# First stage with silu of c on one row and plain column sums; feed-forward and delta net tiles moved to the address of hh modulo 1024

## The chip, the cores and the metric

One core of one Trainium2 chip runs the whole program in one launch. The metric is device time in microseconds (us), the median of the runs of one kernel. Engines are named as the profile names them: PE is TensorE (PEld its weight loads), DVE is VectorE, ACT is ScalarE, POOL is GpSimd, SP is SyncE, whose queue issues nearly all DMAs.

## The reference, cut to what matters

```python
def rms_norm(x, g):
    y = x * lax.rsqrt(jnp.mean(x * x, axis=-1, keepdims=True) + EPS)
    return y * g

def swiglu_ffn(h, w_in, w_out):
    gate, up = jnp.split(h @ w_in, 2, axis=-1)
    return (jax.nn.silu(gate) * up) @ w_out

def reference(x, c, ...):              # x (1, 512, 1024), c (1, 1024), d_ff 2816
    cs = jax.nn.silu(c)
    for i in range(2):
        mod = (cs @ w_ada[i] + b_ada[i]).reshape(B, 3, 3, D)   # shift, scale, gate of three sub-layers
        h = rms_norm(x, norm_g[i, 0]) * (1 + mod[:, 0, 1]) + mod[:, 0, 0]
        x = x + 0.5 * (1 + mod[:, 0, 2]) * swiglu_ffn(h, w_ffn_in[i, 0], w_ffn_out[i, 0])
        h = rms_norm(x, norm_g[i, 1]) * (1 + mod[:, 1, 1]) + mod[:, 1, 0]
        x = x + (1 + mod[:, 1, 2]) * (conv_module(h, ...) if i == 0 else gated_deltanet(h, ...))
        h = rms_norm(x, norm_g[i, 2]) * (1 + mod[:, 2, 1]) + mod[:, 2, 0]
        x = x + 0.5 * (1 + mod[:, 2, 2]) * swiglu_ffn(h, w_ffn_in[i, 1], w_ffn_out[i, 1])
    return rms_norm(x, final_g)
```

## The kernel before, in words

Activations stand transposed: 128 partitions are features, the free axis is the 512 tokens, and the 1024 features are 8 slices `k`. Every product of a large weight is made of three matmuls in fp32r (`mm3`): weight and activation are each split into a high part (`whi`, `hh`) and a remainder (`wlo`, `hl`), and PE adds `whi*hh`, `whi*hl` and `wlo*hh` (lines 172 to 174). Each weight block of 128 columns is loaded by SP into `raw`, cast by ACT into `whi` (line 163), and DVE subtracts to get `wlo` (line 164).

The program has six stages one after the other: feed-forward, convolution module, feed-forward, feed-forward, delta net, feed-forward. In a feed-forward, the pairs of blocks of `w_fi` multiply `hh`, `hl`; their products, split into `ahi` and `alo`, are multiplied by `w_fo` in three groups of 7, 7 and 8 slices (`GROUPS`). The last two of the eight output blocks of the third group, and the head of the next stage, are done in two halves of 256 tokens (`tail`), so that matmuls are 512 or 256 columns wide. The delta net's output product does the same with its tile `ohl`. Inside these stages the order on each engine is the order in which the code is written (`manual_schedule`).

The first stage is written apart (`begin`, and the lines above it). SP loads `c`, `x` in four pieces of two slices, constants, and then for each `k` the rows of the adaLN weights for scale and shift (`load_ada`, two transfers of 512 KB into four places of `stage`) and the first seven weight blocks of slice `k` (`load_st`, 448 KB, two places). The row `c` is multiplied by a column of ones on PE, which lays it on all 128 partitions; ACT takes silu of it into `cs` (128 x 1024). ACT squares the slices of `x`, DVE adds the first six, and PE multiplies the sum and the last two squares by a 128 x 128 matrix of 1/1024 (`mean`), so that each partition has the mean square of each token. ACT takes the square root and DVE the reciprocal of all 128 x 512 elements (`rstd`). For each slice `k` DVE multiplies a row of the adaLN weights by `cs` and sums (`shape`, one call for scale and one for shift), scales `x` (`unit`) and makes the remainders (`low`, `lower`); ACT makes `hh` and its fp32 twin (`high`); and PE runs 21 matmuls into seven accumulators:

```python
        for k in range(KT):
            high(k); cast(k + 1); shape(1, k + 1); low(k); shape(0, k + 1)
            unit(k + 1); lower(k + 1); load(k + 2)
            # 14 matmuls whi, wlo with hh[k], then 7 whi with hl[k]
```

A place in `stage` is loaded anew only when DVE and ACT have read it, and SP takes its DMAs in order. The addresses of tiles are given out by pools in the order in which tiles are asked for. `hh`, `hl` and all slots of `whi` and `wlo` lie at byte 832 modulo 1024 in each partition (a slice of a weight block is 512 bytes, so its slices lie at 832 and 320).

Of the kernel before, what the change touches and what calls it, by code (L numbers as in the profile page):

```python
# [7 lines left out]
F32 = mybir.dt.float32  # L8
F32R = mybir.dt.float32r
BF16 = mybir.dt.bfloat16  # L10
AF = mybir.ActivationFunctionType
ALU = mybir.AluOpType
# [3 lines left out]
P = 128  # L16
T = 512
H2 = T // 2
D = 1024
# [27 lines left out]
NMC = 4  # L47
CT = [3,5]
ARB = 3
SCK = [0,2]  # L50
SNW = 7
NSD = 6
NSH = 3
UMB = 3
HALO=8
# [51 lines left out]
def trunk_kernel(ctx: ExitStack, tc: tile.TileContext, x_in, c_in, vecs, consts, w_ada, w_st,  # L107
# [11 lines left out]
    def nm(s):  # L119
        n_name[0] += 1  # L120
        return f"{s}_{n_name[0]}"
# [4 lines left out]
    def aux_tile():  # L126
        return psum.tile([P, T], F32, tag="ps", name=nm("aux"))

    def scratch(tag, shape=(P, T), dt=F32, bufs=1):
        return sc.tile(list(shape), dt, tag=tag, name=nm(tag), bufs=bufs)  # L130
# [231 lines left out]
            evac(ps, m, full)  # L362

    def preload(func, dep):
        act.activation(scratch("dum", (P, 1)), dep, func, bias=eps, scale=0.0)

    def tok_rstd(pt, n, scale, tag):
        st = scratch(tag, (P, n), bufs=2)
# [10 lines left out]
    def col_sum(pt, src, col0, step=1):  # L379
        for g in range(src.shape[1] // P):  # L380
            pe.matmul(pt[:, col0 + g * step:col0 + g * step + 1], src[:, g * P:(g + 1) * P], ones, start=True, stop=True)
# [109 lines left out]
    def ffn(layer, which, nxt, first=None):  # L491
        sub = 2 * which
        f = layer * 2 + which
        norm = Norm()
        ng = len(GROUPS)
        with tc.tile_pool(name=nm("ffn"), bufs=1) as ap, ExitStack() as ax:
            pump = bool(ada["plan"])
            rate = APACE[which]
            if pump:
                ada["raw"] = ax.enter_context(tc.tile_pool(name=nm("adar"), bufs=2))  # L500
            done = SNW if first else len(edge["w"])
            srcs, starts = [], []
            j0 = 0
            for n in GROUPS:
                starts.append(j0)
                srcs += [(w_fi[f, i], KT) for i in range(max(2 * j0, done), 2 * (j0 + n))]
                srcs += [(w_fo[f, m, :, j0:j0 + n, :], n) for m in range(KT)]
                j0 += n
            srcs += [(s, KT) for s in (nxt[2][:2] if nxt else [])]
            feed = Feed(srcs, [] if first else edge["w"][len(edge["ps"]):], not first)  # L510
            begun = first(f, ap, feed) if first else edge["ps"]
            region = ax.enter_context(ExitStack())
            region.enter_context(tc.manual_schedule(engines=ENG))
            box = {}
            for _ in range(2):
                feed.prep()

            def step(n):
                if pump:
                    ada_step(n)  # L520

            def block(nk, mhi, mlo):
                feed.prep()
                w = feed.take()
                ps = mm_tile()
                for k in range(nk):
                    mm3(ps, w, k, mhi[:, k, :], mlo[:, k, :], k == 0, k == nk - 1)
                return ps

            def glu_a(g):  # L530
                box["s"] = s = scratch("sil", bufs=2)
                act.activation(s, g, AF.Silu)  # L532

            def glu_b(u):
                box["pr"] = pr = scratch("t", bufs=2)
                dve.tensor_tensor(pr, box["s"], u, ALU.mult)  # L536

            def glu_c(jj):
                pr = box["pr"]
                act.copy(ahi[:, jj, :], pr)  # L540
                dve.tensor_tensor(alo[:, jj, :], pr, ahi[:, jj, :].bitcast(F32), ALU.subtract)  # L541

            for gi, n in enumerate(GROUPS):
                ahi = ap.tile([P, n, T], F32R, tag="ahi", name=nm("ahi"))
                alo = ap.tile([P, n, T], F32R, tag="alo", name=nm("alo"))
                for jj in range(n):
                    if len(begun) > 1:
                        g, u = begun.pop(0), begun.pop(0)
                        glu_a(g)
                    else:  # L550
                        g = begun.pop(0) if begun else block(KT, hh, hl)
                        step(rate[0])
                        glu_a(g)
                        u = block(KT, hh, hl)
                        step(rate[1])
                    glu_b(u)
                    glu_c(jj)

                if gi == ng - 1:
                    ev = resid(norm, layer, sub)  # L560
                    for m in range(KT - 2):
                        ps = block(n, ahi, alo)
                        step(rate[2])
                        ev(ps, m, full)
                    if pump:
                        ada_drain(which == 1)
                    tail(None, n, ahi, alo, layer, sub, norm, nxt, feed)
                else:
                    ev = plain_resid(layer, sub)
                    for m in range(KT):  # L570
                        ps = block(n, ahi, alo)
                        step(rate[2])
                        ev(ps, m, full)
# [361 lines left out]
    def deltanet(layer, nxt):  # L935
        NU = HEADS * NG
        norm = Norm()
        with tc.tile_pool(name=nm("dn"), bufs=1) as dp, \
                tc.tile_pool(name=nm("spill"), bufs=1, space=bass.MemoryType.DRAM) as dd:
            kq = dp.tile([P, HEADS, NG, 4, CH], F32, tag="b1", name="kq")  # L940
            kt = dp.tile([P, NG, HEADS, P], F32, tag="b2", name="kt")
            da = dp.tile([P, HEADS, NG, CH], F32, tag="s1", name="da")
            dt = dp.tile([P, HEADS, NG, CH], F32, tag="s2", name="dt")
            am = dp.tile([P, NU, CH], F32, tag="s3", name="am")
            tok = dp.tile([P, NG, 16], F32, name="tok")
            gc = dp.tile([P, HEADS, NG], F32, name="gc")
            egl = dp.tile([P, HEADS, NCH], F32, name="egl")
            kds = dp.tile([P, HEADS, NG], F32, name="kds")
            nbe = dp.tile([P, HEADS, NG], F32, name="nbe")
            beta = dp.tile([P, HEADS, NG], F32, name="beta")  # L950
            ssk = dp.tile([P, HEADS, NG], F32, name="ssk")
# [456 lines left out]
            so = dp.tile([P, 2, HEADS, P], F32, tag="s2", name="so")  # L1408
            S, o0 = so[:, 0], so[:, 1]
            pool.memset(o0[:CH], 0.0)  # L1410
            rms = dp.tile([P, 5, HEADS], F32, name="rms")
            lo_r, hi_r = slice(0, CH), slice(CH, P)

            def oslot(s):
# [132 lines left out]
    orow = ada["pool"].tile([1, P], F32, name="orow", bufs=1)  # L1547
    dve.memset(orow, 1.0)
    nc.sync.dma_start(crow, c_in)
    for k in range(0, KT, 2):  # L1550
        nc.sync.dma_start(x[:, k:k + 2, :], x_in[:, k:k + 2, :])
    nc.sync.dma_start(ident, consts[:, :P])
    nc.sync.dma_start(vec[:, :V1], vecs[:, :V1])
    preload(AF.Silu, eps)
    pcs = [aux_tile() for _ in range(2)]
    for j in range(2):
        pe.matmul(pcs[j], orow, crow[:, j * T:(j + 1) * T], start=True, stop=True)
    mean = ada["pool"].tile([P, P], F32, name="mean", bufs=1)
    dve.memset(mean, 1.0 / D)
    rstd0 = ada["pool"].tile([P, T], F32, name="rstd0", bufs=1)  # L1560
    pt0 = aux_tile()
    sums = scratch("ssum", bufs=1)
    for k in range(KT):
        if k == 0:
            act.activation(sums, x[:, k, :], AF.Square)
        else:
            sq = scratch("sq", bufs=2)
            act.activation(sq, x[:, k, :], AF.Square)
            if k < NSD:
                dve.tensor_tensor(sums, sums, sq, ALU.add)  # L1570
            if k == NSD - 1:
                pe.matmul(pt0, mean, sums, start=True, stop=False)
            if k >= NSD:
                pe.matmul(pt0, mean, sq, start=False, stop=k == KT - 1)
        if k in SCK:
            j = SCK.index(k)
            act.activation(cs[:, j * T:(j + 1) * T], pcs[j], AF.Silu)
            if j:
                preload(AF.Sqrt, cs[:, D - 1:])

    def begin(f, ap, feed):
        stage = ap.tile([P, 4 * D + 2 * SNW * P], F32, tag="ahi", name="stage")
# [31 lines left out]
        def shape(kind, k):  # L1614
            if k < KT:
                c = kind * KT + k
                m = mod[:, 0, c:c + 1]
                junk = ada["raw"].tile([P, D], BF16, tag="ajunk", name=nm("ajunk"), bufs=1)
                dve.tensor_tensor_reduce(junk, adas[kind, k], cs, 1.0, 0.0, ALU.mult, ALU.add, accum_out=m)
                act.activation(m, m, AF.Identity, bias=V("b_ada", c))  # L1620
                if kind:
                    act.activation(gain[:, k:k + 1], m, AF.Identity, scale=V("norm_g", k), bias=V("norm_g", k))

        def unit(k):
            if k < KT:
                xn[k] = scratch("t", bufs=2)
                dve.tensor_tensor(xn[k], x[:, k, :], rstd0, ALU.mult)

        def high(k):
            g, b = gain[:, k:k + 1], mod[:, 0, k:k + 1]  # L1630
# [6 lines left out]

        load(0)
        load(1)
        act.activation(rstd0, pt0, AF.Sqrt, bias=eps)  # L1640
        cast(0)
        dve.reciprocal(rstd0, rstd0)
        unit(0)
        shape(1, 0)
        shape(0, 0)
        ps = [mm_tile() for _ in range(SNW)]
        lower(0)
        for k in range(KT):
# [132 lines left out]
```

## Time and profile before

| | |
|---|---|
| median of 3 runs (lowest, highest) | 2063.96 us (2063.76, 2065.14) |
| the profiled execution's own time | 2064.65 us |
| its span, first to last instruction | 2062.8 us |
| PE busy | 1997.0 us, 97% of the span |
| DVE, ACT, POOL busy | 57%, 38%, 10% |
| first matmul of the first feed-forward | 25.55 us after the span's start |

The profiled execution is one run, 0.69 us above the median. Busy shares are averages over stages; a matmul's listed duration contains its way through the pipeline, so the rate of PE is read from the distance between the starts of matmuls, not from that duration. Of matmuls a few records can be missing.

### The profile page before, as it was taken

Reading aid. Unit: us, or ns where it says so; the run is one execution under the profiler, and the core shown is the slowest. Engines: PE = TensorE matmul, PEld = TensorE weight load, DVE = VectorE, ACT = ScalarE, POOL = GpSimd, SP = SyncE. Lnnn points to the kernel's source line nnn. Section 1 sums busy time; section 2 is a strip of 40 time slices with the busy share of each in tenths; the row PEclk is TensorE's granted clock in tenths of the full one; section 3 lists DMA queues with packets and bytes.
Section 4 is the critical chain, followed back from the end, with each engine's and each line's share of the span. In section 5 each row is a group of like instructions: output and inputs, shape, how many; then the busy total and the mean of one; then the engine's idle time right before and its main releaser. Section 6 shows DMA issues by size and latency. Waiting matters only on the chain.

```text
span 2062.8 us, 26172 instructions
## 1 busy us (share of the span) xinstructions
PE 1997.0 (97%) x10330; PEld 1669.5 (81%) x10330; DVE 1174.2 (57%) x1815; ACT 789.1 (38%) x1357; POOL 198.2 (10%) x139
## 2 busy tenths in 40 slices
PE   6999999998899999999999999999799999999998
PEld 4888888887898888888888888887677798888887
DVE  6766667799865656536333333576745664333334
ACT  5422222475542222224322222377556643222222
POOL 0000000299200000000000000024210100000000
PEclk9999999999899999999999999999999999999999
DMA  7767676322136656532333323322221133333331
GB/s 263 242 219 241 225 237 227 117 82 92 52 112 204 214 182 211 169 99 68 113 99 92 103 93 102 113 72 72 62 63 35 49 113 99 99 98 93 102 93 62
DMA packets 78333, 262.06 MB, mean 127 GB/s; under 512 B 8321, under 2 KB 14081, under 8 KB 78082
## 3 DMA queue, kind: packets, MB, share of 16 engines
q1 hardware_dynamic: 77666, 259.87, 39.6%
q8 instruction: 81, 1.33, 0.3%
q10 hardware_dynamic: 544, 0.52, 0.1%
q14 instruction: 42, 0.34, 0.1%
HBM read 254.59 MB, written 5.77 MB: 126 GB/s over the span
## 4 chain that ended last, share of the span: by engine, by line
PE 87%; DVE 5%; POOL 3%; ACT 3%; issue 2%; DMA 0%; POOLq 0%; DVEq 0%; SPq 0%; ACTq 0%
PE mm L172 26%; PE mm L173 26%; PE mm L174 26%; POOL pacc L671 3%; PE mm L1438 1%; DVE x L1179 1%; PE mm L1460 1%; PE mm L1665 1%; PE mm L1666 1%; PE mm L1446 1%; PE mm L1669 1%; PE mm L1428 1%; DVE x L1184 1%; DVE t L1100 1%; PE aux L376 1%
## 5 line engine op out<-in xcount | busy, mean ns | idle before, releaser
L172 PE MATMUL mm<-hh,whi 128*128 128x512 f32 (+1 forms) x1968 | 742.4, 378 | 6.3 <-ACT hh L273 4.6
L173 PE MATMUL mm<-hl,whi 128*128 128x512 f32 (+1 forms) x1968 | 736.2, 374 | 1.6 <-DVE hl L277 1.3
L174 PE MATMUL mm<-hh,wlo 128*128 128x512 f32 (+1 forms) x1968 | 734.4, 373 | 1.9 <-DVE wlo L164 1.9
L164 DVE TENSOR_TENSOR wlo<-raw,whi 128x1024 fp32r<-128x1024 f32 (+1 forms) x291 | 356.0, 1225 | 305.4 <-ACT whi L163 300.4
L172 PEld LDWEIGHTS mm<-hh,whi 128*128 128x128 f32 x1968 | 371.2, 189 | 74.8 <-ACT hh L273 5.6
L174 PEld LDWEIGHTS mm<-hh,wlo 128*128 128x128 f32 x1968 | 371.7, 189 | 69.0 <-DVE wlo L164 2.9
L173 PEld LDWEIGHTS mm<-hl,whi 128*128 128x128 f32 x1968 | 372.0, 189 | 67.8 <-DVE hl L277 4.0
L163 ACT CAST whi<-raw 128x1024 fp32r<-128x1024 f32 (+1 forms) x291 | 297.3, 1023 | 284.8 <-PE mm L173 257.6
L172 PE MATMUL mm<-ahi,whi 128*128 128x512 f32 (+1 forms) x768 | 288.6, 376 | 0.0
L174 PE MATMUL mm<-ahi,wlo 128*128 128x512 f32 (+1 forms) x768 | 286.6, 373 | 0.0
L173 PE MATMUL mm<-alo,whi 128*128 128x512 f32 (+1 forms) x768 | 284.3, 370 | 0.0
L540 ACT CAST ahi<-t 128x512 fp32r<-128x512 f32 x88 | 54.7, 621 | 371.0 <-DVE t L536 371.0
L174 PEld LDWEIGHTS mm<-ahi,wlo 128*128 128x128 f32 x768 | 144.1, 188 | 28.2
L173 PEld LDWEIGHTS mm<-alo,whi 128*128 128x128 f32 x768 | 144.2, 188 | 27.0
L172 PEld LDWEIGHTS mm<-ahi,whi 128*128 128x128 f32 x768 | 144.4, 188 | 24.2
L425 DVE CUSTOM_DVE_ANT_0 ajunk<-araw,cs 128x1024 bf16<-128x1024 f32 x128 | 156.0, 1219 | 0.6
L532 ACT ACTIVATE sil<-mm 128x512 f32<-128x512 f32 x88 | 52.6, 598 | 255.0 <-PE mm L174 255.0
L536 DVE TENSOR_TENSOR t<-sil,mm 128x512 f32<-128x512 f32 x88 | 60.4, 687 | 142.7 <-PE mm L174 141.0
L469 DVE SCALAR_TENSOR_TENSOR x<-mm,gate,x 128x512 f32<-128x512 f32 x64 | 48.1, 751 | 133.5 <-PE mm L174 133.5
L541 DVE TENSOR_TENSOR alo<-t,ahi 128x512 fp32r<-128x512 f32 x88 | 60.9, 692 | 60.5 <-ACT ahi L540 60.5
L216 POOL TENSOR_TENSOR wlo<-raw,whi 128x1024 fp32r<-128x1024 f32 x6 | 14.4, 2396 | 835.6 <-ACT whi L215 835.6
L671 POOL TENSOR_TENSOR pacc<-pacc,pr 128x492 f32<-128x492 f32 (+11 forms) x58 | 83.2, 1435 | 11.8 <-ACT pr L670 7.6
(263 smaller groups left out, 1681.2 us busy)
## 6 DMA issues: line engine op xcount, KB each, us to landing
raw<-in_w_fi_dram SPq DMA_DIRECT2D x169, 512.0 KB, 3.5
araw<-in_w_ada_dram SPq DMA_DIRECT2D x128, 512.0 KB, 4.5
raw<-in_w_fo_dram SPq DMA_DIRECT2D x64, 448.0 KB, 3.3
raw<-in_w_dn_dram SPq DMA_DIRECT2D x33, 512.0 KB, 3.6
raw<-in_w_fo_dram SPq DMA_DIRECT2D x32, 512.0 KB, 3.5
stage<-in_w_ada_dram SPq DMA_DIRECT2D x16, 512.0 KB, 6.9
raw<-in_w_glu_dram SPq DMA_DIRECT2D x16, 512.0 KB, 3.5
raw<-in_w_pw_dram SPq DMA_DIRECT2D x8, 512.0 KB, 3.7
```

What stands on the lines that cost most here:

```text
L163: act.copy(whi[:, :nk, :], raw[:, :nk, :])
L164: dve.tensor_tensor(wlo[:, :nk, :], raw[:, :nk, :], whi[:, :nk, :].bitcast(F32), ALU.subtract)
L172: pe.matmul(ps, whi[:, k, :], mhi, start=first, stop=False)
L173: pe.matmul(ps, whi[:, k, :], mlo, start=False, stop=False)
L174: pe.matmul(ps, wlo[:, k, :], mhi, start=False, stop=last)
L425: dve.tensor_tensor_reduce(junk, raw, ada["cs"], 1.0, 0.0, ALU.mult, ALU.add, accum_out=mod[:, layer, col:col + 1])
L469: dve.scalar_tensor_tensor(x[:, m, sl], ps, gate[:, j:j + 1], x[:, m, sl], ALU.mult, ALU.add)
L532: act.activation(s, g, AF.Silu)
L536: dve.tensor_tensor(pr, box["s"], u, ALU.mult)
L540: act.copy(ahi[:, jj, :], pr)
L541: dve.tensor_tensor(alo[:, jj, :], pr, ahi[:, jj, :].bitcast(F32), ALU.subtract)
L671: pool.tensor_tensor(pacc[m][:, c], pacc[m][:, c], pr[:, c], ALU.add)
```

## The change: what it does

**First stage.** `c` is put through silu on its own row (1 x 1024) before PE spreads it, and DVE copies the two results out of PSUM into `cs`. The load of the table for Sqrt comes right behind that silu. `x` comes in five pieces (1, 1, 2, 2, 2 slices). All eight squares go into one sum on DVE (seven additions), with six buffers in turn instead of two. PE takes column sums of it by four matmuls of one column each (`col_sum`), so that a token's sum stands on its own partition; square root and reciprocal are of 128 x 4 elements; and four matmuls with the identity (`spread`) lay the result on all partitions in a PSUM tile `pb0`, which `unit` reads. In DVE's order `shape(1, 0)` now stands ahead of the reciprocal and `shape(0, 0)` ahead of `unit(0)`. 15 matmuls on a tile of zeros in bf16 (`wrm`) are added, 4 ahead of the product with `c`, 7 behind it and 4 behind `spread`; their result is not read.

**Addresses.** A pad tile in each feed-forward pool, and three small tiles of the delta net moved ahead of its large ones, change where tiles lie. In the built programs, `ahi`, `alo`, the delta net's `ohl`, `kq`, `kt` and the first stage's `stage` and `wst` lie at 128 modulo 1024 before and at 832 after. The weights' slots, `hh` and `hl` stay at 832. The convolution's tiles move too, but to no such place.

```diff
-SCK = [0,2]
-NSD = 6
+PAD = (40, 168)
+XP = ((0, 1), (1, 1), (2, 2), (4, 2), (6, 2))
+WARM = (4, 7, 4)
...
         with tc.tile_pool(name=nm("ffn"), bufs=1) as ap, ExitStack() as ax:
+            ap.tile([P, PAD[layer]], F32, tag="pad", name=nm("pad"))
...
+            rms = dp.tile([P, 5, HEADS], F32, name="rms")
+            gc = dp.tile([P, HEADS, NG], F32, name="gc")
+            egl = dp.tile([P, HEADS, NCH], F32, name="egl")
+            kds = dp.tile([P, HEADS, NG], F32, name="kds")
             kq = dp.tile([P, HEADS, NG, 4, CH], F32, tag="b1", name="kq")
...
     preload(AF.Silu, eps)
+    wrm = ada["pool"].tile([P, T], BF16, name="wrm", bufs=1)
+    pool.memset(wrm, 0.0)
     pcs = [aux_tile() for _ in range(2)]
+    pt0, pw = aux_tile(), aux_tile()
+    def warm(i):
+        for _ in range(WARM[i]):
+            pe.matmul(pw, wrm[:, :P], wrm, start=True, stop=True)
+    warm(0)
+    act.activation(crow, crow, AF.Silu)
+    preload(AF.Sqrt, crow[:, D - 1:])
     for j in range(2):
         pe.matmul(pcs[j], orow, crow[:, j * T:(j + 1) * T], start=True, stop=True)
+    warm(1)
...
-            sq = scratch("sq", bufs=2)
+            sq = scratch(("sq", "t", "sil")[k % 3], bufs=2)
             act.activation(sq, x[:, k, :], AF.Square)
-            if k < NSD:
-                dve.tensor_tensor(sums, sums, sq, ALU.add)
-            if k == NSD - 1:
-                pe.matmul(pt0, mean, sums, start=True, stop=False)
-            if k >= NSD:
-                pe.matmul(pt0, mean, sq, start=False, stop=k == KT - 1)
-        if k in SCK:
-            j = SCK.index(k)
-            act.activation(cs[:, j * T:(j + 1) * T], pcs[j], AF.Silu)
-            if j:
-                preload(AF.Sqrt, cs[:, D - 1:])
+            dve.tensor_tensor(sums, sums, sq, ALU.add)
+    col_sum(pt0, sums, 0)
+    for j in range(2):
+        dve.tensor_copy(cs[:, j * T:(j + 1) * T], pcs[j])
...
-                dve.tensor_tensor(xn[k], x[:, k, :], rstd0, ALU.mult)
+                dve.tensor_tensor(xn[k], x[:, k, :], pb0, ALU.mult)
...
-        act.activation(rstd0, pt0, AF.Sqrt, bias=eps)
+        st0 = scratch("rst4", (P, NG))
+        act.activation(st0, pt0[:, :NG], AF.Sqrt, bias=eps, scale=1.0 / D)
         cast(0)
-        dve.reciprocal(rstd0, rstd0)
+        shape(1, 0)
+        dve.reciprocal(st0, st0)
+        pb0 = spread([st0[:, g:g + 1] for g in range(NG)])
+        warm(2)
+        shape(0, 0)
         unit(0)
-        shape(1, 0)
-        shape(0, 0)
```

On DVE, from the additions of squares (`ssum`) to the first remainder of weights (`wst`), the order before is this (`ajunk` is the product of `shape`, the line behind it reads out its sum; `t` is the result of `unit`):

```order
L1570 TENSOR_TENSOR ssum_105<-ssum_105,sq_123 128x512
L1642 RECIPROCAL rstd_103<-rstd_103 128x512
L1627 TENSOR_TENSOR t_150<-x,rstd_103 128x512
L1619 ISA ajunk_152,mod<-stage,cs 128x1024
L1619 ISA mod 128x1
L1619 ISA ajunk_156,mod<-stage,cs 128x1024
L1619 ISA mod 128x1
L1612 TENSOR_TENSOR wst<-stage,wst 128x896
```

and of the change this (`aux_100` and `aux_101` are `c` on all partitions, `aux_172` is `pb0`):

```order
L1580 TENSOR_TENSOR ssum_120<-ssum_120,t_140 128x512
L1583 COPY cs<-aux_100 128x512
L1583 COPY cs<-aux_101 128x512
L1623 ISA ajunk_167,mod<-stage,cs 128x1024
L1623 ISA mod 128x1
L1648 RECIPROCAL rst_18_164<-rst_18_164 128x4
L1623 ISA ajunk_181,mod<-stage,cs 128x1024
L1623 ISA mod 128x1
L1631 TENSOR_TENSOR t_184<-x,aux_172 128x512
L1616 TENSOR_TENSOR wst<-stage,wst 128x896
```

The two copies came in, the reciprocal went from 512 columns to 4 and behind the first `shape`, and `unit` went behind the second.

On ACT, from the program's start to the first cast of weights, the order before has both silu of 128 x 512 and the second table load among the squares:

```order
L365 ACTIVATE dum_95<-eps 128x1
L1565 ACTIVATE ssum_105<-x 128x512
L1577 ACTIVATE cs<-aux_97 128x512
L1568 ACTIVATE sq_108<-x 128x512
L1568 ACTIVATE sq_111<-x 128x512
L1577 ACTIVATE cs<-aux_98 128x512
L365 ACT_TABLE_LOAD
L365 ACTIVATE dum_115<-cs,eps 128x1
L1568 ACTIVATE sq_117<-x 128x512
```

and of the change the silu of one row and the table load ahead of all squares:

```order
L367 ACTIVATE dum_96<-eps 128x1
L1568 ACTIVATE crow<-crow 1x1024
L367 ACT_TABLE_LOAD
L367 ACTIVATE dum_109<-crow,eps 1x1
L1576 ACTIVATE ssum_120<-x 128x512
L1579 ACTIVATE t_122<-x 128x512
L1579 ACTIVATE sil_125<-x 128x512
L1579 ACTIVATE sq_128<-x 128x512
```

The squares now stand together, with nothing between them. Behind the first stage no engine's order differs.

## Rows read from the trace of the kernel before

**Rows 1.** The page: busy time by engine, and the last chain by engine.

```profile
PE 1997.0 (97%) x10330; PEld 1669.5 (81%) x10330; DVE 1174.2 (57%) x1815; ACT 789.1 (38%) x1357; POOL 198.2 (10%) x139
...
PE 87%; DVE 5%; POOL 3%; ACT 3%; issue 2%; DMA 0%; POOLq 0%; DVEq 0%; SPq 0%; ACTq 0%
```

**Rows 2.** Windows: stretch, length, busy (count) by engine, granted clock, DMA share, GB/s.

```profile
4.00:10.00 6.00, 2.02 (x3) 0.33 (x1) 1.39 (x2) 4.76 (x9) 0.00 (x0) 1.00 1.01 387
17.10:25.55 8.45, 0.00 (x0) 0.00 (x1) 7.65 (x8) 3.35 (x7) 0.00 (x0) 0.65 0.13 39
25.55:29.82 4.27, 4.27 (x10) 3.40 (x11) 4.27 (x8) 3.27 (x7) 0.00 (x0) 0.50 0.92 316
29.82:66.79 36.97, 36.97 (x160) 29.77 (x159) 31.62 (x47) 25.06 (x43) 0.00 (x0) 1.00 0.78 270
```

**Rows 3.** Chain in order of time, first 26 us: start, us, what.

```profile
1.15 4.04 DMA x<-in_x_in_dram
...
12.35 2.08 PE aux L1572 x2
14.42 2.66 PE aux L1574 x4
...
17.83 3.36 DVE rstd L1642
...
24.68 0.82 ACT hh L1631
25.55 0.80 PE mm L1665
```

**Rows 4.** Timeline, first 13 us: start, us, engine, instruction, count, [idle before, releaser].

```profile
2.27 3.75 PE L1557 MATMUL aux<-crow,orow 1*128 1x512 f32 x4 [2.27 <-DMA crow<-in_c_in_dram]
...
7.87 1.28 ACT L365 ACT_TABLE_LOAD   x1
...
10.01 2.29 DVE L1570 TENSOR_TENSOR ssum<-ssum,sq 128x512 f32<-128x512 f32 x3 [1.64 <-ACT sq L1568]
```

**Rows 5.** Timeline of DVE and ACT, 24 to 60 us.

```profile
24.24 1.09 DVE L1612 TENSOR_TENSOR wst<-stage,wst 128x896 fp32r<-128x896 f32 x1
...
37.78 1.22 DVE L1619 CUSTOM_DVE_ANT_0 ajunk<-stage,cs 128x1024 bf16<-128x1024 f32 x1 [1.71 <-DMA stage<-in_w_ada_dram]
...
59.16 0.82 ACT L1631 ACTIVATE hh<-t,mod,gain 128x512 fp32r<-128x512 f32 x1 [0.37 <-DVE t L1627]
```

**Rows 6.** Timeline of PE: where runs of 512-wide matmuls begin.

```profile
32.49 0.40 PE L1665 MATMUL mm<-hh,wst 128*128 128x512 f32 x1
...
66.79 0.39 PE L172 MATMUL mm<-hh,whi 128*128 128x512 f32 x1
...
104.88 0.40 PE L172 MATMUL mm<-ahi,whi 128*128 128x512 f32 x1
...
143.35 0.40 PE L172 MATMUL mm<-hh,whi 128*128 128x512 f32 x1
```

**Rows 7.** Timeline of PE: first and last of two runs 256 wide.

```profile
378.10 0.28 PE L172 MATMUL mm<-ahi,whi 128*128 128x256 f32 x1
...
386.11 0.28 PE L174 MATMUL mm<-ahi,wlo 128*128 128x256 f32 x1
...
580.75 0.28 PE L174 MATMUL mm<-hh,wlo 128*128 128x256 f32 x1
...
586.50 0.28 PE L174 MATMUL mm<-hh,wlo 128*128 128x256 f32 x1
```

**Rows 8.** Groups by line: count | busy us, mean ns | idle before, releaser.

```profile
L1449 DVE COPY so<-mm 128x128 f32<-128x128 f32 x8 | 1.8, 284 | 4.6 <-PE mm L1446 4.6
L881 DVE RECIPROCAL rs<-vr 128x4 f32<-128x4 f32 x1 | 0.2, 179 | 0.4 <-ACT vr L878 0.4
L376 PE MATMUL aux<-cst,rst 128*128 128x128 f32 x48 | 7.4, 276 | 0.6 <-DVE rst L262 0.6
L381 PE MATMUL aux<-ones,ssum 128*128 128x1 f32 x48 | 6.2, 233 | 3.3 <-DVE ssum L405 3.3
L1438 PE MATMUL mm<-sq,rm 64*64 64x128 f32 x112 | 19.0, 284 | 0.0
```

More of the change, by code (lines that the diff above doesn't have):

```diff
@@ L364, in preload @@
     def preload(func, dep):
-        act.activation(scratch("dum", (P, 1)), dep, func, bias=eps, scale=0.0)
+        n = dep.shape[0]
+        act.activation(scratch("dum", (P, 1))[:n], dep, func, bias=eps[:n], scale=0.0)
     def tok_rstd(pt, n, scale, tag):
@@ L945, in deltanet @@
             tok = dp.tile([P, NG, 16], F32, name="tok")
-            gc = dp.tile([P, HEADS, NG], F32, name="gc")
-            egl = dp.tile([P, HEADS, NCH], F32, name="egl")
-            kds = dp.tile([P, HEADS, NG], F32, name="kds")
             nbe = dp.tile([P, HEADS, NG], F32, name="nbe")
@@ L1410, in deltanet @@
             pool.memset(o0[:CH], 0.0)
-            rms = dp.tile([P, 5, HEADS], F32, name="rms")
             lo_r, hi_r = slice(0, CH), slice(CH, P)
@@ L1549, in trunk_kernel @@
     nc.sync.dma_start(crow, c_in)
-    for k in range(0, KT, 2):
-        nc.sync.dma_start(x[:, k:k + 2, :], x_in[:, k:k + 2, :])
+    for k, n in XP:
+        nc.sync.dma_start(x[:, k:k + n, :], x_in[:, k:k + n, :])
     nc.sync.dma_start(ident, consts[:, :P])
@@ L1554, in trunk_kernel @@
     preload(AF.Silu, eps)
+    wrm = ada["pool"].tile([P, T], BF16, name="wrm", bufs=1)
+    pool.memset(wrm, 0.0)
     pcs = [aux_tile() for _ in range(2)]
+    pt0, pw = aux_tile(), aux_tile()
[5 more added lines that the diff above has]
+    preload(AF.Sqrt, crow[:, D - 1:])
     for j in range(2):
         pe.matmul(pcs[j], orow, crow[:, j * T:(j + 1) * T], start=True, stop=True)
[L1558 to L1561, printed above, removed]
+    warm(1)
     sums = scratch("ssum", bufs=1)
```

## The prediction, as made before the result was known

> **What bounds the kernel now.** I read the page first: PE is busy 97% of the span and holds 87% of the last chain [rows 1], so time is won only where PE starts earlier, waits less, or runs its matmuls closer together. Then the windows of the beginning: from 17.10 to 25.55 us PE does nothing, from 25.55 to 29.82 it runs 10 matmuls at a granted clock of 0.50 (1.2 GHz, 427 ns apart), and from 29.82 on it is busy without a gap at 1.00 (2.4 GHz) [rows 2]. Then the chain through those first 25 us: arrival of x, squares, PE's two products with `mean` (12.35 to 17.08), the reciprocal of 512 columns (3.36 us), `shape` twice, `hh`, first matmul at 25.55 [rows 3]. Last the timeline of PE for the distance between starts of matmuls. From 66.79 to 104.88 us stand 7 blocks of 24 matmuls with `hh` and `hl`: 38.09 us / 168 = 226.7 ns each. From 104.88 to 143.35 stand 8 blocks of 21 with `ahi` and `alo`: 38.47 / 168 = 229.0 ns. From 32.49 to 66.79 stand the first stage's slices 1 to 7, 147 matmuls with `hh` against `wst`: 34.30 / 147 = 233.3 ns [rows 6]. All are the same instruction of the same size, and none waits; they differ in the place modulo 1024 (really modulo 512, since slices of weights step by 512): `hh` and its weights both at 832, `ahi` at 128 against weights at 832, `hh` at 832 against `wst` at 128.
>
> **First stage: when does the first matmul start?** Silu of the row: `c` is there at 2.27 [rows 4], an ACT pass over 1024 columns is about 1.0 us (twice the 0.5 of a square of 512), then a table load of 1.28 [rows 4] and a preload of 0.3: ACT is free at about 4.9. The first x piece lands at 5.19 [rows 3], half of it now a little earlier, so this costs nothing while x is under way; without that cover it would cost 2.6. The remaining 1.57 MB of x at 387 GB/s [rows 2] take 4.1 us: x is complete at 9.3. Squares of 0.6 follow each piece; the six buffers remove ACT's waits for DVE. DVE's seven additions at 0.76 (2.29 for three [rows 4]) run from the third on without a break from 7.1: they end at 11.6. Against before, two more additions replace five microseconds of PE.
>
> Behind that on DVE: two copies of 512 columns (0.28 for 128 [rows 8]; I take 0.65 each), ending at 12.9; `shape(1, 0)` 1.22 and its read-out 0.08 [rows 5], ending at 14.2. The column sums (8 records, 6.2 / 48 = 0.13 each [rows 8], 1.0 us) and the root lie beside them on PE and ACT. Reciprocal 0.18 [rows 8]: 14.4. `spread`: 8 records at 7.4 / 48 = 0.15 [rows 8], with the way through the pipeline 1.3: 15.7, and `shape(0, 0)` beside it, also 15.7. `unit(0)` 0.6: 16.4. `hh` 0.82 [rows 3]: 17.2. First matmul at about **17.3** instead of 25.55, 8.2 us sooner. Bounds: 16.8 if copies and `spread` are as fast as their shortest parts, 18.2 if PE runs `spread` at half clock and x's extra DMA delays all loads behind it by its 0.45 us of issue.
>
> **First stage: when does it end?** Three paces. PE: 168 matmuls, `wst` now at 832 against `hh` at 832, so 226.7 ns instead of 233.3 (1.1 us less): 38.1 us, which from 17.3 ends at 55.4. Low clock: before, ten matmuls cost 427 instead of 233, 2.0 us [rows 2]. PE has idled 8.45 us ahead of them; after, it has four matmuls and `spread` just ahead of the first, but idles about 2 us at 9 and at 12.6 us, so I leave 0 to 2.0 open: 55.4 to 57.4. DVE with the loads: `lower(0)` begins at 24.24 before [rows 5], after at 16.4, 7.9 sooner. From there the loop of DVE, SP and DMA is the same; before, it made the last `hh` at 59.98 [rows 5], with a wait of 1.71 for a transfer [rows 5]. So `hh(7)` comes at 52.1, and 21 matmuls of 226.7 (4.8) end at 56.9. I take 56.9 to 57.4, against 66.79: **9.5 us** gained. Loads are then the closest limit: two more waits as long as the one of 1.71 make it 6.1; none at all with a full clock makes it 11.4. The 15 matmuls on zeros cost nothing: the first 11 run while ACT and DVE work on x, the last 4 (0.9, at half clock 1.7) while `unit` and `hh` run (1.5); without that cover they would be on the path. Next in line, the first blocks of `w_fi` come through SP, ACT and DVE with the same 7.9 us, and PE needs three blocks (16 us) before a late fourth could stop it.
>
> **Addresses.** `ahi`, `alo` against `whi`, `wlo`, all at 832, are then exactly what `hh`, `hl` are now, so I take that row: 226.7 instead of 229.0. Four feed-forwards with 160 output blocks of slices each run 640 x 3 = 1920 such matmuls: 2.3 x 1920 = 4.4 us less, and 48 of `ohl` 0.1 less. But 256 wide it goes the other way: 68 steps with `ahi` take 8.01 us, 117.8 ns; 48 with `hh`, 5.75 us, 119.8 ns [rows 7]. 384 of `ahi` and 288 of `ohl` lose 2.0 each: 1.4 us more. Net **3.1 us** less. Nothing in the rows shows what the new places do to DVE, ACT or the delta net's fp32 matmuls; their tiles keep their distances among each other, so 0, with 1 us to either side. The bounds of the part are 0, if the place is not the cause, and 4.4, if the 256-wide ones don't lose.
>
> The Trainium skill (SBUF — State Buffer, "SBUF: two separate sides") says that on the engine side only the pair of ports shared by DVE and GpSimd causes contention, and that PE never waits on anyone. By that, an address could not change a matmul's pace, and the sum would be about 3.1 us smaller, with 1.1 less from `wst`. The 226.7, 229.0 and 233.3 [rows 6] speak against it, but they are three tiles and not one tile moved.
>
> **Sum.** 9.5 + 3.1 = 12.6. The profiled execution took 2064.65 (span 2062.8 and 1.85 around it), so 2052.0; it stood 0.69 above the median, which gives 2063.96 - 12.6 = **2051.4**.
>
> **The rivals.**
> - *The place is not the cause.* The tiles differ in more than their address (`wst` has its own order of matmuls). Then `wst` stays at 233.3: PE ends the first stage at 56.6 to 58.6, gain 8.5, and nothing else changes: 2055.5. The identical order of `ahi` and `hh` blocks speaks against it.
> - *Loads set the first stage.* Stretch 29.82 to 66.79 moves 270 GB/s at a DMA share of 0.78 [rows 2], and a slice's 1.5 MB at that rate take 5.6 us, more than PE's 4.8. Against it: DVE lost only 1.71 in one place, and gaps in the traffic are places of `stage` not yet free. Gain 6.1 + 3.1: 2054.8.
> - *The change does not do what it says.* The early start is lost again, because the last slices land when they did before; 3.1 and no more than 1 remain: 2060 or above, no measurable change.
> - *Slower.* The delta net's chunk loop waits on each of its small fp32 matmuls; their operands (`kq`, `kt`, `rm`, `pm`) move to 832 while others (`sq`, `sil`) stay at 864. The products with `rm` already take 19.0 / 112 = 170 ns [rows 8]. About 480 such records lie in the loop: from 26 ns more on each the 12.6 are eaten, and at 50 ns more the time is 2063.96 - 12.6 + 24 = 2075. Before, these tiles had a worse mixture of places, and nothing points to it but ignorance.
>
> The Trainium skill (TensorE: Matmul & The Clock Gate, Part 1) says that the slow clock is the rest state and that matmul activity releases it. By that the 15 matmuls would save the whole 2.0; the trace agrees so far that the slow stretch follows an idle one [rows 2], and here the loads would take most of it back, so the sum stays.
>
> **How the numbers follow.** Forecast 0.64 (its own range 2048.5 to 2054.5), place not the cause 0.10, loads 0.15, no change 0.06, slower 0.05. The range of 8 in 10 reaches from the largest first-stage gain with all of the address gain (11.4 + 4.4, 2048, and half a microsecond more) to the loads' case with no address gain (2063.96 - 6.1 = 2057.9, less 1 as both together are unlikely): 2047.5 to 2057. Faster by over 0.2% (4.1 us, about what a measurement of this kernel tells from no change) is 0.89, within it 0.06, slower 0.05.
>
> **What would show it.** First matmul at 17 to 18 us on PE's timeline, last of the first stage at 57; DVE's waits for `stage` not above 3 us together; `ahi` runs at 227 ns and 120 ns (256 wide), `wst` at 227; the stretch of the delta net as long as before (1399 to 1636). The prediction is wrong if the first stage ends after 60 us, if `ahi` keeps its 229, or if the delta net or the convolution changes by over 2 us.

## The result, and the profile after

The changed kernel takes 2051.73 us (median of 6 runs, 2051.14 to 2053.78) against 2063.86 (6 runs, 2063.44 to 2065.14): ratio 0.9942, 95% interval 0.9929 to 0.9955, 12.1 us less where 12.6 were forecast. The execution profiled below took 2053.78 us, 2.05 above the median, the slowest of the six; no other one of them was profiled, so where the 2.05 lie is not shown.

The page of the changed kernel: PE is still the bound, with the share of the chain that it had [rows 1].

```profile
PE 1999.5 (97%) x10355; PEld 1676.0 (82%) x10355; DVE 1173.2 (57%) x1818; ACT 788.8 (38%) x1356; POOL 198.6 (10%) x140
...
PE 87%; DVE 5%; POOL 3%; ACT 3%; issue 2%; DMA 0%; SPq 0%; DVEq 0%; POOLq 0%; ACTq 0%
```

Its timeline from 8 to 22 us (the answer to [rows 3, 4]), with the way to the first matmul:

```profile
8.80 0.63 ACT L1579 ACTIVATE sil<-x 128x512 f32<-128x512 f32 x1 [2.85 <-DMA x<-in_x_in_dram]
...
14.06 1.28 DVE L1583 COPY cs<-aux 128x512 f32<-128x512 f32 x2
...
14.19 1.87 PE L383 MATMUL aux<-ones,ssum 128*128 128x1 f32 x8 [3.99 <-DVE ssum L1580]
...
16.75 2.07 PE L378 MATMUL aux<-cst,rst 128*128 128x128 f32 x8 [0.69 <-DVE rst L1648]
...
19.64 0.81 ACT L1635 ACTIVATE hh<-t,mod,gain 128x512 fp32r<-128x512 f32 x1 [1.44 <-DVE t L1631]
...
20.51 0.79 PE L1672 MATMUL mm<-hh,wst 128*128 128x512 f32 x1
...
21.10 0.63 PE L1673 MATMUL mm<-hh,wst 128*128 128x512 f32 x1
```

ACT waits 2.85 us for the third slice of x; the copies behind the sums start at 14.06 and not at 11.6. Copies, column sums and `spread` follow in the order of the forecast, the last two in 1.87 and 2.07 us where I had 1.0 and 1.3. The first matmul is at 20.51. The first starts are 0.59 and 0.43 us apart, half clock; from 22.34 on they are 0.227 apart on average.

The windows of the changed kernel (columns as in [rows 2]). PE has no pause from 20.51 to 59.56, so PE and not the loads sets the end of the first stage: 39.05 us for its 168 matmuls instead of 41.24.

```profile
14.20:20.51 6.31, 5.62 (x20) 4.04 (x21) 5.29 (x10) 2.83 (x7) 0.00 (x0) 1.00 0.71 258
...
22.30:59.56 37.26, 37.26 (x165) 30.79 (x164) 33.44 (x50) 26.26 (x45) 0.00 (x0) 1.00 0.80 291
```

(The clock column shows 1.00 up to the first change that the trace records, here at 22.27; ahead of it the distance of the starts tells the clock.)

PE's timeline at the places of [rows 6]: an `ahi` run of 168 takes 135.72 - 97.64 = 38.08 us, 226.7 ns each, as the `hh` run ahead of it does.

```profile
59.56 0.39 PE L173 MATMUL mm<-hh,whi 128*128 128x512 f32 x1
...
97.64 0.39 PE L173 MATMUL mm<-ahi,whi 128*128 128x512 f32 x1
...
135.72 0.39 PE L173 MATMUL mm<-hh,whi 128*128 128x512 f32 x1
```

From the starts on PE's timelines, in us, for the kernel before, the changed one and three of the experiments. "conv" goes from the convolution's first 512-wide matmul to the end of the `hh` run behind it, "delta net" from its first 512-wide matmul to the first 512-wide one with `ohl` (156 with `ohl` that are 256 wide lie in it):

| stretch | before | after | places only | stage only | four pieces |
|---|---|---|---|---|---|
| start to first matmul | 25.55 | 20.51 | 25.15 | 19.66 | 18.15 |
| first stage | 41.24 | 39.05 | 40.14 | 40.27 | 38.30 |
| one `ahi` run of 168, of 8 | 38.47 | 38.08 | 38.08 | 38.47 | 38.08 |
| conv | 268.40 | 268.78 | 267.21 | 267.22 | 268.42 |
| delta net | 320.87 | 320.29 | 320.45 | 326.81 | 320.13 |
| last instruction's end | 2062.77 | 2051.99 | 2055.29 | 2061.33 | 2047.35 |

### The profile page after: what moved, and what is told of

It reads as the page before. It is cut to its first block, busy times and chain, and to the rows that moved or that the text cites. A ratio compares the mean times of both kernels' runs of the same rounds, so it can differ in the third digit from the quotient of the medians.

```text
span 2052.0 us, 26228 instructions
## 1 busy us (share of the span) xinstructions
PE 1999.5 (97%) x10355; PEld 1676.0 (82%) x10355; DVE 1173.2 (57%) x1818; ACT 788.8 (38%) x1356; POOL 198.6 (10%) x140
## 4 chain that ended last, share of the span: by engine, by line
PE 87%; DVE 5%; POOL 3%; ACT 3%; issue 2%; DMA 0%; SPq 0%; DVEq 0%; POOLq 0%; ACTq 0%
PE mm L173 26%; PE mm L174 26%; PE mm L175 26%; POOL pacc L674 3%; PE mm L1441 1%; PE mm L1463 1%; DVE x L1183 1%; PE aux L378 1%; PE mm L1449 1%; PE mm L1672 1%; PE mm L1673 1%; PE mm L1676 1%; PE mm L1431 1%; DVE t L1104 1%; DVE x L1188 1%
```

## The experiments

**Places alone, stage alone.** The kernel before with the new places:

```
-(no pad in the ffn pool)          +ap.tile([P, PAD[layer]], F32, ...)   # PAD = (176, 176)
-rms, gc, egl, kds behind the rest +rms, gc, egl, kds first, and 8 floats of pad
```

> The kernel before with the new places alone: the feed-forward's and the delta net's tiles stand at the same address modulo 1024 as hh, the first stage is the old one. Nothing is left out of the computation. Theory (the place sets the pace): the eight groups of 168 matmuls with ahi and alo take 38.08 us each instead of 38.47, the first stage's matmuls with wst 226.7 ns instead of 233.3, the 256-wide ones 120 instead of 118; together 3.1 us from the feed-forwards and about 1 us from the first stage, so about 2060 us against 2063.9 (ratio 0.998). Rival (the place is not the cause, and all of the gain comes out of the first stage): paces of 229.0 and 233.3 as before, 2063.9, ratio 1.000. If the delta net's stretch is 0.9 us shorter here too, the new places of its tiles are the cause of that, otherwise not.

2057.18 us (5 runs, 2056.71 to 2057.99) against 2065.18: ratio 0.9963 (0.9950 to 0.9977). Its PE timeline has the pace:

```profile
65.29 0.39 PE L173 MATMUL mm<-hh,whi 128*128 128x512 f32 x1
...
103.37 0.39 PE L173 MATMUL mm<-ahi,whi 128*128 128x512 f32 x1
...
141.45 0.39 PE L173 MATMUL mm<-hh,whi 128*128 128x512 f32 x1
```

The rival is out: nothing but addresses changed, the `ahi` runs went from 38.47 to 38.08 and the first stage with `wst` from 41.24 to 40.14. Yet the gain is 7.5 in the profile, not 4. Of it 1.1 is `wst`, 3.1 the eight `ahi` runs, 0.4 the eight `hh` runs (76.21 to 76.16 and 87.09 to 87.04), 0.9 the last part of each feed-forward; that is 5.5. The rest is 1.2 in conv, 0.4 ahead of the first matmul and 0.4 in the delta net. The 1.2 go with the clock: ahead of a stretch of 17.1 us at half clock that all fourteen profiles have in conv, six, this one among them, have it once for 6.8 us and take 267.1 to 267.7 us for conv; the other eight, among them those before and after, have it twice for 3.4 us and take 268.4 to 269.8.

The delta net is shorter here too: 293.86 us before, 293.10 here and 292.94 after, up to its first matmul with `ohl`. The expectation took that for the mark of the places; but the kernel below with these tiles at 160 has 292.73, so equal addresses are not what does it, and the cause stays open. (The tiles moved to the front are four, not three: `rms`, `gc`, `egl`, `kds`.)

The other half: the changed kernel with the tiles back at 128.

```
-PAD = (40, 168)                   +PAD = (120, 0)
-rms, gc, egl, kds first           +at their old places
-st0 = scratch("rst4", ...)        +st0 = ada["pool"].tile(...)
```

> The changed kernel with its first stage, but the tiles back at the old places (128 modulo 1024). Nothing is left out of the computation. Theory: the first matmul at 18 to 20.5 us, the matmuls with wst at about 233 ns again, ahi and alo at 229.0, so that 8 to 9 us of the 12 are won: about 2055.5 us, ratio 0.996 against the kernel before. The sum of this gain and of the one with the places alone should be that of the whole change, 12.1, within about 1. Rival (the place is not the cause): all of the gain is here, 2051.7, ratio 0.994.

2064.67 us (11 runs, 2062.12 to 2066.73): ratio 0.9992 (0.9983 to 1.0002), no gain that can be told, against both theories. The first stage is not the reason: it ends at 59.94, 6.85 sooner than before, and the delta net begins 8.0 sooner. There 5.9 are lost. The windows of this kernel in the delta net, and below them the same place before:

```profile
1495.00:1515.00 20.00, 18.85 (x416) 15.09 (x411) 8.70 (x14) 13.43 (x25) 2.57 (x2) 1.00 0.34 106
1515.00:1535.00 20.00, 20.00 (x91) 16.48 (x91) 6.78 (x23) 6.75 (x25) 0.94 (x1) 0.66 0.02 2
```

```profile
1503.00:1523.00 20.00, 18.58 (x415) 15.11 (x409) 8.72 (x14) 13.43 (x25) 2.55 (x2) 1.00 0.38 107
1523.00:1543.00 20.00, 19.99 (x117) 14.44 (x116) 8.09 (x28) 8.94 (x29) 2.84 (x2) 1.00 0.09 27
```

The order of work is the same, but behind 20 us of small matmuls that end with a pause of PE (1.15 us, for the last `sil` of the v side) the granted clock is 0.66 in place of 1.00, and 91 matmuls stand in the stretch in place of 117. The trace has half clock (1.2 GHz) for 13.7 us from 1516.9 on, in which 6.8 us of work at full clock are done. The pause alone does not bring it about: the changed kernel and the one with four pieces below have it at the same place, 1.15 us long, without the fall.

So 8.0 and 0.5 do not add up to the 12.1 of the whole change. With the 5.9 given back, and conv's 1.2 of clock taken from both halves, the estimate is 12.0.

**Five matmuls for the pause.** If the pause has a part in it, matmuls put there should give the 6 us back:

```
 z_fill(ZF)
-tr(p)
+tr(p, 5)     # first: pe.matmul(pt, hh[:, 0, :P], hh[:, 0, :], ...) 5 times
```

> The kernel with the new first stage and the old places, and five more matmuls of hh by itself (5 times 0.227 us, their result is overwritten and read by nothing) in the delta net, in the pause of 1.15 us ahead of the last transposes of v, behind which the clock fell to 0.66 of a 20 us stretch. Theory (the gain of the first stage is there in full, and the fall of the clock behind that pause gave 6 us of it back): no fall there, the delta net's stretch at about 321 us instead of 326.8, and 2057 to 2059, ratio about 0.997. Rival (the delta net is longer for another reason, a wait or a place): the stretch stays at 326 to 327, and the time at 2064.7 or a little above.

2061.29 us (12 runs, 2057.01 to 2067.55), ratio 0.9978 (0.9965 to 0.9990). Nine of the twelve have a mean clock of 0.988 to 0.990 and took 2057.0 to 2062.1; two have 0.984 and 0.985 and took 2067.5; the twelfth has 0.986 and took 2062.7. One of the two was profiled, with the fall at the same place:

```profile
1515.00:1535.00 20.00, 19.28 (x72) 15.40 (x73) 5.38 (x20) 3.71 (x12) 0.95 (x1) 0.57 0.00 1
```

But the five are not in the pause. PE's timeline there has them ahead of three more matmuls, and the pause is as long as it was:

```profile
1512.57 1.31 PE L1124 MATMUL aux<-hh 128*128 128x512 f32 x5
1513.71 0.39 PE L173 MATMUL mm<-hh,whi 128*128 128x512 f32 x1
...
1515.72 0.66 PE L1127 MATMUL aux<-cst,sil 128*128 128x128 f32 x4 [1.17 <-ACT sil L1118]
```

All eleven runs without the five had 0.984 to 0.986. So 1.1 us more of matmuls ahead of the pause make the fall rare, as far as the mean clock of runs without a profile tells, and the fall costs about 6 us; where it falls is decided by little. What a filled pause would do was not tested. The kernel before seems to have the fall too: of 17 runs beside this experiment four, at 0.983 and 0.984, took 2070.7 to 2072.8, and the others 2063.4 to 2066.5; none of the four was profiled. The runs at the full clock stay 2 us above the 2057 to 2059 that I expected; the five matmuls, which no pause hid, can be 1.1 of that, and the rest is not explained.

**Five pieces or four.** The profile after showed x late.

```
-XP = ((0, 1), (1, 1), (2, 2), (4, 2), (6, 2))
+XP = ((0, 2), (2, 2), (4, 2), (6, 2))
```

> The changed kernel with x loaded in four pieces of two slices, as before, instead of five. Nothing is left out of the computation. Theory (x landed late in the profile of the changed kernel, at 11.40 us instead of 9.26, because that execution was one of the slower, not because of the five pieces): the same within 0.4 us, 2051.7. Rival (the fifth transfer and its issue delay x by 2 us): x complete at 9.3, the first matmul at 18 to 18.5 instead of 20.5, and 2 us faster: 2049.7. A third outcome: 0.5 to 1 us slower, since the first square has to wait for 512 KB instead of 256.

2049.34 us (5 runs, 2048.30 to 2051.82), ratio 0.9927 (0.9914 to 0.9939): the rival is right, my theory of an unlucky execution wrong. Timeline, then the window from 3 to 7 us:

```profile
6.41 0.63 ACT L1579 ACTIVATE sil<-x 128x512 f32<-128x512 f32 x1
...
18.15 0.57 PE L1672 MATMUL mm<-hh,wst 128*128 128x512 f32 x1
...
18.55 0.39 PE L1673 MATMUL mm<-hh,wst 128*128 128x512 f32 x1
18.78 0.40 PE L1672 MATMUL mm<-hh,wst 128*128 128x512 f32 x1
...
56.45 0.39 PE L173 MATMUL mm<-hh,whi 128*128 128x512 f32 x1
```

```profile
3.00:7.00 4.00, 3.80 (x5) 1.16 (x4) 0.69 (x1) 3.67 (x7) 0.00 (x0) 1.00 1.00 365
```

The same window of the changed kernel:

```profile
3.00:7.00 4.00, 3.88 (x5) 1.16 (x4) 0.69 (x1) 2.92 (x5) 0.00 (x0) 1.00 0.94 295
```

All profiles of the new first stage agree: in the seven with five pieces the third square starts at 6.94 to 8.80 us, the stretch moves 295 to 331 GB/s and the first matmul comes at 18.92 to 20.51; in the five with four pieces it is 6.17 to 6.67, 365 to 377 GB/s and 17.94 to 18.46. Why two transfers of 256 KB slow the ones behind them was not tested.

**The matmuls on zeros**, taken away from the changed kernel and from the one with four pieces:

```
-WARM = (4, 7, 4)
+WARM = (0, 0, 0)
```

> The changed kernel without the 15 matmuls on zeros, whose result nothing reads. Theory (they bring the clock up sooner): the first matmuls of the first stage run at the granted clock of 0.50 for longer, about 10 of them at 427 ns as in the kernel before instead of the 4 in the changed kernel, so 6 times 0.2 = 1.2 us slower, 2.0 at the most: 2052.9 to 2053.7. Rival (PE is not what sets the end of the first stage, its loads are): no difference, 2051.7, the late start being made up by the end of the stage at 59.6 us.

2051.89 us (5 runs, 2050.24 to 2054.05), 0.9938 (0.9925 to 0.9950): no difference in the time, while the first stage took 39.98 us instead of 39.05. The 0.9 is near the theory's 1.2. In the profile x was less late (third square at 7.05), which makes up for it; that execution is the fastest of its five, 2050.24, so why the medians are level is not shown.

> The changed kernel with x in four pieces and without the 15 matmuls on zeros, whose result nothing reads. Theory (with x on time they have the clock up when the first stage's matmuls begin: the first intervals were 409, 229 and 233 ns): without them some 8 matmuls at 427 ns, 1.6 us slower than with the four pieces, 2050.5 to 2051. Rival (the loads set the end of the first stage, as far as x is on time): no difference, 2049.3.

2051.56 us (5 runs, 2050.34 to 2053.11), 0.9931 (0.9918 to 0.9945); first stage 39.73 instead of 38.30. Timeline:

```profile
17.94 0.80 PE L1672 MATMUL mm<-hh,wst 128*128 128x512 f32 x1 [1.69 <-ACT hh L1635]
18.53 0.63 PE L1673 MATMUL mm<-hh,wst 128*128 128x512 f32 x1
18.96 0.63 PE L1672 MATMUL mm<-hh,wst 128*128 128x512 f32 x1
```

Behind an idle stretch of 1.69 us the matmuls start 0.43 apart, and the trace has the granted clock rise at 21.18; with the zeros ahead it rises at 18.33, and they start 0.23 apart from 18.55 on (rows above). The 1.4 us in the stage are near the theory's 1.6. The medians differ by 2.2; what is more than the 1.2 at the end of the stage (57.67 against 56.45) lies behind it and was not followed up.

**Distance and pace.** Three kernels with other pads move the feed-forwards' tiles by some bytes against the weights, each layer by its own:

```
-PAD = (40, 168)
+PAD = (56, 200)    # 64 and 128 bytes;  (104, 264): 256 and 384;  (152, 176): 448 and 32
```

> The changed kernel with the feed-forward's tiles moved on by 64 bytes in the first feed-forward and by 128 in the second, against the weights, which stay. Nothing is left out of the computation. Theory (what counts is the distance between the place of the moving operand and that of the weights modulo 512): the pace of the matmuls with ahi and alo differs from 226.7 ns and differs between the two feed-forwards; known are 226.7 at a distance of 0 and 229.0 at one of 320; a distance at which it comes below 226.7, towards the 216 or so that 512 columns take at 2.4 GHz, is possible and would be worth up to 10 ns on some 8,700 matmuls. The first stage's matmuls with wst move by the same 64. Rival (only the absolute place counts, or equal places are the best): 226.7 or more in both, and the whole time at 2051.7 to 2056.

> As the kernel with 64 and 128 bytes, with 256 in the first feed-forward and 384 in the second. Nothing is left out of the computation. Theory: the pace of ahi and alo is a function of the distance modulo 512, between 224 and 236 ns; 256 and 384 lie on both sides of the 320 of the kernel before (229.0), so both near 229 unless the function is narrow. Rival: no smooth dependence; the pace is 226.7 or 229 in both.

> As the kernel with 64 and 128 bytes, with 448 in the first feed-forward and 32 in the second. Nothing is left out of the computation. Theory: 448 is 64 behind the weights' place, 32 just ahead of it; if the function is narrow around 0 then both differ from 226.7, in opposite senses perhaps. Rival: both 226.7 to 227, since they are near the distance of 0.

PE's timelines, starts of an `ahi` run and of the run behind it, in the first and in the second layer. 64 and 128 bytes:

```profile
96.45 0.40 PE L173 MATMUL mm<-ahi,whi 128*128 128x512 f32 x1
...
134.92 0.40 PE L173 MATMUL mm<-hh,whi 128*128 128x512 f32 x1
...
1028.43 0.40 PE L173 MATMUL mm<-ahi,whi 128*128 128x512 f32 x1
...
1067.63 0.39 PE L173 MATMUL mm<-hh,whi 128*128 128x512 f32 x1
```

256 bytes:

```profile
96.21 0.39 PE L173 MATMUL mm<-ahi,whi 128*128 128x512 f32 x1
...
134.29 0.39 PE L173 MATMUL mm<-hh,whi 128*128 128x512 f32 x1
```

448 bytes:

```profile
97.05 0.39 PE L173 MATMUL mm<-ahi,whi 128*128 128x512 f32 x1
...
136.25 0.39 PE L173 MATMUL mm<-hh,whi 128*128 128x512 f32 x1
```

With the kernels before and after:

| distance, bytes | modulo 256 | 168 matmuls, us | ns each |
|---|---|---|---|
| 0, 256 | 0 | 38.08 | 226.7 |
| 64, 320 | 64 | 38.47 | 229.0 |
| 32 | 32 | 39.20 | 233.3 |
| 128, 384 | 128 | 39.19 | 233.3 |
| 448 | 192 | 39.20 | 233.3 |

The period is 256 and not the 512 of my theory, 0 is the best place tried, and three of the five take the same 233.3, also that of `wst` before. Lines of the second layer with 384 bytes, then with 32:

```profile
1024.38 0.40 PE L173 MATMUL mm<-ahi,whi 128*128 128x512 f32 x1
...
1063.58 0.39 PE L173 MATMUL mm<-hh,whi 128*128 128x512 f32 x1
```

```profile
1031.24 0.40 PE L173 MATMUL mm<-ahi,whi 128*128 128x512 f32 x1
...
1070.45 0.40 PE L173 MATMUL mm<-hh,whi 128*128 128x512 f32 x1
```

But the distance is not all. In these kernels `wst` moves too, against an `hh` that stays. With `hh` at a distance of 192 modulo 256 from it (64 bytes) a matmul takes 233.3 ns, with 0 (256 bytes) 226.7, as in the table. With 64 (448 bytes) there are two paces in one stage: PE's starts, one slice or 21 matmuls apart, go from 4.90 us (233.3 ns) to 4.81 (229.0) at about 39.7 us, at the same addresses, without a pause and at a granted clock of 1.00:

```profile
28.31 1.80 PE L1676 MATMUL mm<-hl,wst 128*128 128x512 f32 x7
33.21 1.80 PE L1676 MATMUL mm<-hl,wst 128*128 128x512 f32 x7
...
42.95 1.76 PE L1676 MATMUL mm<-hl,wst 128*128 128x512 f32 x7
47.76 1.76 PE L1676 MATMUL mm<-hl,wst 128*128 128x512 f32 x7
```

What else has a part in the pace is open. The whole times, one run each, were 2060.20, 2057.59 and 2070.63 (the last with the delta net's clock fall: 327.31 us there).

**The same for `hh`.** If the distance alone counts, it must hold for the tiles that make most of the matmuls:

```
 x = keep.tile([P, KT, T], F32, name="x")
+gain = keep.tile([P, DEPTH * 3 * KT], F32, name="gain")   # 192 bytes, from behind mod
 hh = keep.tile([P, KT, T], F32R, name="hh")
```

> The changed kernel with x in four pieces, and hh and hl moved on by 192 bytes, everything else where it was (a tile of 192 bytes, the gains, now stands ahead of them instead of behind). Nothing is left out of the computation. Theory (it is the distance between the moving operand and the weights modulo 256, whatever the tile): the blocks with hh and hl take 39.20 us per 168 matmuls instead of 38.08, as those with ahi did at a distance of 448, and those with ahi stay at 38.08. 4944 matmuls 512 wide at 6.6 ns more make 32.6 us, the 168 with wst 1.1; the 960 that are 256 wide win 3 to 4 ns each, 3 to 4 us: 2049.3 and 30 make 2079, at least 2074. Rival (the pace of ahi in the runs before came from ahi's own place or tile): 38.08 for hh too, and 2049.3.

2080.16 us (4 runs, 2076.44 to 2082.27), ratio 1.0072 (1.0055 to 1.0089): 31 us slower than with four pieces, the theory's 30. The `hh` run takes 39.20, the `ahi` run 38.10:

```profile
58.13 0.39 PE L173 MATMUL mm<-hh,whi 128*128 128x512 f32 x1
...
97.33 0.40 PE L173 MATMUL mm<-ahi,whi 128*128 128x512 f32 x1
...
135.43 0.39 PE L173 MATMUL mm<-hh,whi 128*128 128x512 f32 x1
```

**The delta net's places, and its pause.** On the kernel with four pieces:

```
-rms, gc, egl, kds first           +at their old places (ohl, kq, kt at 160)
```

> The changed kernel with x in four pieces, and the delta net's tiles back at their old places (128 modulo 1024), the feed-forward's tiles at the new ones. Nothing is left out of the computation. Theory (what the delta net's places change is the 288 matmuls with ohl that are 256 wide, 118 ns at the old place and 120 at the new one, and the 48 that are 512 wide, 229 and 227): 0.5 us faster than with the four pieces alone, 2048.8, so not to be told from no change; that stretch of the delta net as long as before within 0.5. Rival (the 0.5 to 0.9 us that the delta net's stretch was shorter in the changed kernel come from its places): 0.5 to 0.9 slower, 2050. If the clock falls behind the pause ahead of the last transposes of v, 6 to 7 us slower by that alone.

2050.78 us (5 runs, 2049.94 to 2052.18), 0.9928 (0.9914 to 0.9941), that is the 0.9927 of the new places; delta net 320.12 against 320.13 us. The tiles came to stand at 160 and not at 128, 96 modulo 256 from the weights; the stretch of the `ohl` matmuls took 0.3 us more, not 0.5 less, which is 233.3 ns for its 48 that are 512 wide. Of the 1.4 us between the medians 0.8 stand at the end of the first stage in the profiles (57.23 against 56.45). So no gain of the delta net's places can be told; the old place itself was not tried here.

```
-ZF = 1
+ZF = 3
```

> The changed kernel with x in four pieces, and with three of the delta net's z steps instead of one ahead of the last transposes of v: work that is done later anyway is put into the pause of 1.15 us there. Nothing is left out of the computation. Theory (PE sets the delta net's time): 0.7 to 1.2 us faster than with the four pieces alone, 2048.2 to 2048.7. Rival (the scan behind it then lacks these two steps, 1.36 us, where PE waits for it): no gain, 2049.3, or up to 1 us slower.

2052.86 us (6 runs, 2051.62 to 2055.68), 0.9939 (0.9924 to 0.9953): slower by more than the rival said. The pause is still 1.2 us, so the chain ahead of it moved too, and the delta net takes 323.3 us instead of 320.1; 1.7 of these are a new stretch of 3.4 us at half clock at 1626. Where the rest went was not settled.

## Why the prediction was right

The time was right to 0.3 us, in part by luck: the first stage gave 2.3 less than forecast, the rest gave some 0.5 more in the profiles, and the medians lie 1.3 further apart than the profiles. The steps:

- **First stage, 9.5 us: too large for this kernel.** Measured 7.2 in the profile, and 6.9 to 8.7 in the other six with five pieces. The step that failed is the arrival of x: the prediction had it come at 387 GB/s and be complete at 9.3, and let the extra piece cost 0.45 us of issue at most. It came at 295 GB/s from 3 to 7 us, the third square waited 2.85 us (0.9 to 2.9 in the seven), and the last two squares began at 11.42, against 9.04 with four pieces. With four pieces the rest of that working nearly holds: first matmul at 18.15 against 17.3, end at 56.45 against 56.9, 10.3 us won. `spread` at half clock, 0.8 more than I took, is nearly all of the lateness that is left; the column sums took 0.9 more, but beside DVE's copies and `shape`.
- **Which limit ends the stage.** I took the loads; it was PE, which had no pause from first to last, at 226.7 ns a matmul and with four at half clock, of the ten before. The bound "0 to 2.0" for the low clock holds: against 168 matmuls at 226.7 ns (38.08 us) the stage took 1.0 more here, 0.2 with four pieces and 1.6 with four pieces and no zeros.
- **Addresses, 3.1 us: right in kind, too small.** `ahi` 226.7, `wst` 226.7 and 120 for the 256-wide ones [rows 6, 7] came as forecast, but the places alone give about 5.1 with `wst`, where 3.1 and 1.1 stood: the `hh` runs won 0.05 each and the last parts 0.2 each, and `ohl` lost 0.4 where 0.5 stood (70.35 us to 70.74 from its first matmul to the next stage's first 512-wide one).
- **The errors nearly cancel.** The first stage gave 7.2, the addresses behind it 3.9 and the delta net ahead of `ohl` 0.9, whose cause is open. Conv takes 0.4 back, and 0.9 more are lost, nearly all of it at the end, where half clock comes 2.1 us ahead of the end of PE's last matmul (2043.0, 2045.14) and before came behind it (2057.3, 2056.03): 10.8 between the two profiles, 12.1 between the medians. This execution has the latest third square of the seven profiles with five pieces, 8.80, and that early half clock at the end; that these are the missing 1.3 is not shown.
- **The rivals.** "The place is not the cause" fell with the kernels that move addresses alone. The Trainium skill (SBUF — State Buffer, "SBUF: two separate sides") has PE never waiting on anyone; what the prediction drew from that, that an address could not change a matmul's pace, does not hold here: `ahi` moved by some bytes takes 226.7 to 233.3 ns. "Loads set the first stage" fell by PE's unbroken stretch. "Slower" named the delta net and the wrong mechanism: the places of its tiles cost nothing that can be told, but its clock can fall, at a price of 6 us, enough to hide the whole first stage when this half of the change is made alone. The profile before showed nothing of that price, since its clock was 1.00 there.

## What to carry to other kernels

Compare the start-to-start distance of matmuls of one size among their tiles: if it differs, put moving operand and weights at equal addresses modulo 256 and measure again, since up to 3% of each 512-wide matmul hung on it here; for 256-wide ones the equal place was the slowest. Look at the granted clock of both kernels by stretch before a small difference is put down to the edit: a gain of 8 us was gone in a stretch that nobody had touched. A load on the path is not improved by a smaller first piece unless the pieces behind it are as early as before. And look in the trace where matmuls that were added to fill a pause come to stand.

## What the runs showed that I had not expected

- The pace of a 512-wide fp32r matmul took three values, by the distance modulo 256 of its moving operand from the weights: 226.7 ns at 0, 229.0 at 64, 233.3 at 32, 96, 128 and 192, with one stretch at 64 that ran at 233.3 and then at 229.0. Of 256-wide ones 120 ns at 0 was the slowest seen; at 64 and at 192 both 117.8 and 113.3 occurred.
- Two transfers of 256 KB in place of one of 512 KB at the head of a queue: 295 to 331 GB/s from 3 to 7 us, instead of 365 to 377.
- Behind one and the same pause of some 1.15 us the clock fell in the profiles of three kernels (first stage alone, the same with five matmuls more, 448 and 32 bytes) and of no other; by the mean clock, in all eleven executions of the first and two or three of twelve of the second. The delta net took 326.8 us in the first, against 320.3 in the changed kernel.
